# Output projection of the cross-attention by seven products of eight, with block sums of its inputs and its results read back

## The chip, the cores and the metric

The kernel runs on one core of a Trainium2 chip. The metric is the device time of one execution in microseconds. TensorE (PE) multiplies, VectorE (DVE) and ScalarE (ACT) work element by element, GpSimd (POOL) issues some DMAs through its queue and SyncE (SP) issues most of the others. Each engine works through its own queue in order. Activations lie in a shared set of 66 slots in SBUF.

## What is computed

One layer of a hybrid decoder for 512 prompt tokens and 8 single-token samples, 520 columns in all, in float32 with a model width of 2048:

```python
y = mixer(rmsnorm(x, g_mix));          x = x + y          # ends in  @ w_out
q = rmsnorm(x, g_xattn) @ w_cq
o = softmax(q @ mk.T * 512**-0.5) @ mv                    # 4 heads, 256 memory tokens
x = x + o @ w_co                                          # the projection that is changed
x = x + square(relu(rmsnorm(x, g_ffn) @ w_up)) @ w_down
y = rmsnorm(x, g_final)
```

## The kernel before

Columns are tokens (`T` = 520, two halves of `HT` = 260); a tile holds 128 rows of the width, so x is 16 tiles (`KB` = 16). A float32 factor is split into a high and a low part, and each product is three matmuls: high by high, high by low, low by high. A weight tile of 128x1024 (eight 128x128 blocks) is loaded on SP into `wraw`, cast on ACT into `whi` (L129, or L138 in stretches written by hand), and `wlo` = `wraw` - `whi` is made on DVE (L130, L146). `run_jobs` (L164) goes through a list of jobs: it loads the weights of later jobs, splits those of the job after next and then issues the matmuls, with the result's step behind them (`post`).

A plain product (`gemm`, L189) makes a 128x520 tile of results out of 16 input tiles: two jobs of 48 matmuls, 260 columns wide. A quad (`quad_jobs`) makes two such tiles, seen as 2x2 blocks (two input parities by two column halves, two output tiles by two halves), by seven products of eight: sums of weight blocks (`S1` to `S4`, four 128x1024 steps on DVE, L1256), seven products P1 to P7 of 24 matmuls each, and an addition of each product into the results. Its inputs are blocks and sums of blocks of two activation tiles each; those sums are made ahead and split, and part of them is kept in DRAM and loaded at use.

The program in order: the input projection, the mixer; `w_out` as one plain pair (`out_plain`) and seven quads (`out_quad`), whose results go to DRAM (`dx[0]`) and are read back and split (`x1_again`); `w_cq`; then products for keys (`mk_jobs`, L1050) and values (`mv_jobs`, L1081) of four heads, between which the attention of each head (`attn`, L1150) is interleaved, in an order written by hand (`tc.manual_schedule`); `w_co` (`residual`, L858, 16 plain products); the feed-forward with one plain pair, 31 quads of `w_up` and the quads of `w_down`. The cached keys and values of the samples are loaded on POOL and multiplied on DVE meanwhile (L962, L969).

In `attn` each of a head's four outputs lies in PSUM; ACT casts it to `oh` and DVE makes `ol` (L1160). `residual` reads its x tile from `dx[0]`, adds the product (L871), stores it to `dx[1]` and hands it to `fact_out`, which splits it for the up stage (`fa`, L801) and, for every two tiles, makes block sums (L1195) and their split (L1230), stored to `td`. The first two tiles are put off (`put_off`) until the pools of the early stages are closed.

## Time and profile before

| | us |
|---|---|
| runs | 2667.88, 2674.22, 2666.63 (median 2667.88) |
| profiled run, and its span | 2668.74, 2667.0 |
| PE busy in the span | 2639.8 (99%) |
| DVE busy | 2135.2 (80%) |
| ACT busy | 1253.2 (47%) |
| last mk and mv jobs and the attention of the heads | about 943 to 1195 |
| w_co | 1170.2 to 1359.1 |
| up stage's quads | 1383.0 to 2003.7 |

A part of an engine's time counts for the whole only where the others wait for it. So one looks first which engine is busy throughout, then at what it waits for, and then, for another engine, how much it has to do in the stretch in which it gets new work.

### The profile page before, as it was taken

To read this page: it belongs to the slowest core of one execution; us is meant where nothing else is said; L and a number is where in the kernel's file an instruction comes from. 1 tells how busy PE (TensorE), PEld (TensorE's weight loads), DVE (VectorE), ACT (ScalarE), POOL (GpSimd) and SP (SyncE) were. 2 spreads that over 40 slices of the span, in tenths; PEclk is the share of its full clock that TensorE was granted. 3 is DMA by queue.
4 is the path that set the end of the run, shared out by engine and by line. 5 is a ranking of instruction groups with operands and counts; after the bars stand their busy time and mean duration, and the time that the engine had idled before them with its cause. 6 is when DMAs were issued, how large, how long until landed. Compare 5 with 4: busy or idle time off the path is not lost.

```text
span 2667.0 us, 52574 instructions
## 1 busy us (share of the span) xinstructions
PE 2639.8 (99%) x21418; PEld 2602.9 (98%) x21418; DVE 2135.2 (80%) x3593; ACT 1253.2 (47%) x1704; POOL 108.3 (4%) x184
## 2 busy tenths in 40 slices
PE   9999999999999999999999999999999999999997
PEld 9999999999999999989999999999999999999997
DVE  6786786897865567775569999999999998998898
ACT  5646364553453144444445555555553333333344
POOL 0010000000001212110000000000000000000001
PEclk9999999999999999999999999999999999999999
DMA  5354443566456778775566565565579666555642
GB/s 205 105 191 135 124 162 105 177 220 235 141 180 200 274 264 279 264 243 192 184 226 228 195 211 196 190 210 198 189 245 335 217 219 219 180 172 191 212 131 89
DMA packets 236068, 528.91 MB, mean 198 GB/s; under 512 B 24638, under 2 KB 96990, under 8 KB 235826
## 3 DMA queue, kind: packets, MB, share of 16 engines
q1 hardware_dynamic: 216882, 458.43, 51.1%
q0 software_dynamic: 18944, 67.12, 7.3%
q8 instruction: 168, 2.75, 0.4%
q14 instruction: 74, 0.61, 0.1%
HBM read 426.27 MB, written 99.33 MB: 197 GB/s over the span
## 4 chain that ended last, share of the span: by engine, by line
PE 91%; issue 4%; DVE 2%; DMA 2%; ACT 1%; POOL 0%; SPq 0%; POOLq 0%; DVEq 0%; ACTq 0%
PE mm L1286 46%; PE mm L203 29%; PE mm L1050 3%; PE mm L1081 3%; PE aux L222 3%; PE aux L1286 2%; PE mm L1329 2%; DVE wlo L130 1%; PE aux L657 1%; DMA wraw<-in_w_in 1%; PE aux L728 0%; PE aux L661 0%; DMA hc<-r 0%; PE aux L654 0%; DMA wraw<-in_w_mv 0%
## 5 line engine op out<-in xcount | busy, mean ns | idle before, releaser
L129 ACT CAST whi<-wraw 128x1024 fp32r<-128x1024 f32 x396 | 416.0, 1051 | 730.1 <-PE mm L1286 388.2
L1286 PE MATMUL mm<-ha,whi 128*128 128x260 f32 x3584 | 643.5, 283 | 1.9 <-ACT whi L129 1.0
L130 DVE TENSOR_TENSOR wlo<-wraw,whi 128x1024 fp32r<-128x1024 f32 x396 | 483.1, 1220 | 151.3 <-ACT whi L129 149.2
L1286 PEld LDWEIGHTS mm<-ha,whi 128*128 128x128 f32 x3584 | 551.0, 188 | 2.8 <-DVE X L1455 1.3
L1286 PE MATMUL mm<-ha,wlo 128*128 128x260 f32 x1792 | 505.0, 282 | 0.6 <-DVE wlo L130 0.6
L1286 PE MATMUL mm<-ta,whi 128*128 128x260 f32 x2320 | 419.3, 283 | 0.0
L1286 PEld LDWEIGHTS mm<-ta,whi 128*128 128x128 f32 x2320 | 356.2, 188 | 0.0
L1286 PEld LDWEIGHTS mm<-ha,wlo 128*128 128x128 f32 x1792 | 337.0, 188 | 1.0 <-DVE wlo L130 1.0
L1286 PE MATMUL mm<-ta,wlo 128*128 128x260 f32 x1160 | 326.8, 282 | 0.0
L1286 PE MATMUL mm<-fa,whi 128*128 128x260 f32 x1488 | 268.3, 282 | 0.0
L203 PE MATMUL mm<-xh,whi 128*128 128x260 f32 x1280 | 264.2, 287 | 0.9 <-DVE og L775 0.9
L203 PE MATMUL mm<-xl,whi 128*128 128x260 f32 x1280 | 259.9, 284 | 0.0
L203 PE MATMUL mm<-xh,wlo 128*128 128x260 f32 x1280 | 257.8, 282 | 0.0
L1286 PEld LDWEIGHTS mm<-fa,whi 128*128 128x128 f32 x1488 | 228.1, 188 | 0.0
L129 ACT CAST whi<-A 128x1024 fp32r<-128x1024 f32 x126 | 132.3, 1050 | 185.6 <-PE mm L1286 120.2
L138 ACT CAST whi<-wraw 128x1024 fp32r<-128x1024 f32 x100 | 105.1, 1051 | 243.5 <-PE mm L203 84.6
L1286 PEld LDWEIGHTS mm<-ta,wlo 128*128 128x128 f32 x1160 | 218.4, 188 | 0.0
L1286 PE MATMUL mm<-fa,wlo 128*128 128x260 f32 x744 | 209.2, 281 | 0.0
L1455 DVE TENSOR_TENSOR X<-mm,X 128x260 f32<-128x260 f32 x448 | 170.6, 421 | 41.4 <-PE mm L1286 39.5
L203 PEld LDWEIGHTS mm<-xh,whi 128*128 128x128 f32 x1280 | 198.4, 188 | 2.3 <-ACT kv L825 1.0
L203 PEld LDWEIGHTS mm<-xh,wlo 128*128 128x128 f32 x1280 | 198.5, 189 | 0.2
L203 PEld LDWEIGHTS mm<-xl,whi 128*128 128x128 f32 x1280 | 198.0, 189 | 0.3
(420 smaller groups left out, 5093.9 us busy)
## 6 DMA issues: line engine op xcount, KB each, us to landing
ha<-hc SPq DMA_DIRECT2D x224, 260.0 KB
wraw<-in_w_in SPq DMA_DIRECT2D x80, 512.0 KB
wraw<-in_w_up SPq DMA_DIRECT2D x66, 512.0 KB
wraw<-in_w_down SPq DMA_DIRECT2D x64, 512.0 KB
A<-in_w_down SPq DMA_DIRECT2D x64, 512.0 KB
A<-in_w_up SPq DMA_DIRECT2D x62, 512.0 KB
hc<-hhi SPq DMA_DIRECT2D x32, 910.0 KB
hc<-r SPq DMA_DIRECT2D x32, 910.0 KB
```

What stands on the lines that cost most here:

```text
L129: S.copy(hi, raw)
L130: V.tensor_tensor(out=lo, in0=raw, in1=hi.bitcast(F32), op=ALU.subtract)
L138: S.copy(hi, raw)
L203: PE.matmul(ps[:, hf, 0:HT], w[:, j, :], x[:, HALF[hf]], start=(k == 0 and wi == 0), stop=(k == n - 1 and wi == 2))
L222: PE.matmul(out, u, v, start=first and i == 0, stop=last and i == 2)
L657: PE.matmul(nps[:, ms], C[j][:, ms], qs[j][:, cs], start=False, stop=(j == 1))
L1050: PE.matmul(box["ps"], w[:, i, :], x, start=(k == 0 and wi == 0), stop=(k == KB - 1 and wi == 2))
L1081: PE.matmul(box["ps"][:, i], x[:, ms], w[:, j], start=(k == 0 and wi == 0), stop=(k == KB - 1 and wi == 2))
L1286: PE.matmul(out, w[:, j, :], x[:, b], start=(new and k == 0 and wi == 0), stop=(p == LAST[acc] and k == per - 1 and wi == 2), skip_group_c ...
L1329: PE.matmul(ps[mp][:, hf, 0:HT], w[:, j, :], x[hf][:, b], start=(kp == 0 and j == 0 and wi == 0), stop=(kp == 1 and j == 7 and wi == 2))
L1455: V.tensor_tensor(out=x, in0=c, in1=x, op=ALU.add)
```

## The change

`w_co` becomes `projection("w_co", ...)`, the form that `w_out` has already: one plain pair and seven quads. `out_plain`, `out_quad`, `x1_again` and `residual` are replaced by it.

- The heads' outputs are copied from PSUM to a slot `o` on ACT and split by halves into `fo` (`block_out`). Tiles are paired across heads 0 and 1, and 2 and 3. For the four pairs of heads 0 and 1 `o_sums` makes four differences of blocks and their high and low parts and stores them on POOL into `od`, 16 stores; `o_loads` loads them again. For the four pairs of heads 2 and 3 `o_loads` makes the differences and splits them into `to` at the start of the first quad.
- The small SBUF pool is closed two jobs earlier, and the loads of the first quad's four weight tiles (`held`) are issued behind that.
- The results go to `dx[1]`; 14 of the 16 are read back in the last quad, split (`fact_split`), and summed by pairs (`fact_pair`).
- `w_out`'s plain pair reads its inputs in another order, and the weights are packed on the host for both.

```diff
+    def block_diffs(d1, d3, d2, d4, t0, t1):
+        b12, b11, b21, b22 = t0[:, HALF[1]], t0[:, HALF[0]], t1[:, HALF[0]], t1[:, HALF[1]]
+        for out, p, q in ((d1, b12, b11), (d2, b22, d1), (d3, b22, b12), (d4, b21, d2)):
+            V.tensor_tensor(out=out, in0=p, in1=q, op=ALU.subtract)
...
+    def block_out(t, n):
+        fo[n] = [pair_slot("fo") for _ in range(2)]
+        for hf in range(2):
+            split_to(fo[n][hf], t[:, HALF[hf]])
+        if n % 2 == 0:
+            o_even[n // 2] = t
+        elif n < 8:
+            start(o_sums(n // 2, o_even.pop(n // 2), t))
+        else:
+            o_last.append((n // 2, o_even.pop(n // 2), t))
+
+    def o_sums(i, t0, t1):
+
+        yield
+        u, w = slot("ou", (P, 2, HT)), slot("ou", (P, 2, HT))
+        block_diffs(u[:, 0], u[:, 1], w[:, 0], w[:, 1], t0, t1)
+        for k, t in ((0, u), (2, w)):
+            yield
+            hi = pair_slot("oh")
+            S.copy(hi, t)
+            V.tensor_tensor(out=t.bitcast(F32R), in0=t, in1=hi.bitcast(F32), op=ALU.subtract)
+            for b, x in enumerate((hi.bitcast(F32), t)):
+                stream_load(odram[i][k:k + 2, :, b].rearrange("j p c -> p j c"), x)
+
+    def o_loads():
+
+        for i in range(KB // 2):
+            to[i][1], to[i][2], to[i][3] = fo[2 * i][0], fo[2 * i + 1][0], fo[2 * i + 1][1]
+        for j in (6, 4, 5, 7):
+            if j in (6, 4):
+                for i, t0, t1 in o_last[0:2]:
+                    u, w = slot("ou", (P, 2, HT)), slot("ou", (P, 2, HT))
+                    block_diffs(u[:, 0], u[:, 1], w[:, 0], w[:, 1], t0, t1)
+                    for k, x in ((6, w[:, 0]), (4, u[:, 0]), (5, u[:, 1]), (7, w[:, 1])):
+                        to[i][k] = pair_slot("to")
+                        split_to(to[i][k], x)
+                del o_last[0:2]
+            for i in range(len(odram)):
+                to[i][j] = pair_slot("to")
+                load(to[i][j].bitcast(F32), odram[i][j - 4])
+            yield
...
-                hi, lo = slot("oh", dt=F32R), slot("ol", dt=F32R)
-                for src, c in ((op, slice(0, TP)), (od[:, 4 * h + j - 2], DEC)):
-                    S.copy(hi[:, c], src)
-                    V.tensor_tensor(out=lo[:, c], in0=src, in1=hi[:, c].bitcast(F32), op=ALU.subtract)
-                oact.append((hi, lo))
+                t = slot("o")
+                S.copy(t[:, 0:TP], op)
+                S.copy(t[:, DEC], od[:, 4 * h + j - 2])
+                parts.append((t, 8 * (h // 2) + 2 * (j - 2) + h % 2))
...
+    def projection(wname, src, dst, key, facts, tacts, done, again, early):
...
+        def x_done(n):
+            load(dst[n], xs[n])
...
+            if n >= KB - 2:
+                again(xs[n], n)
+            if n % 2:
+                done(n // 2, xs[n - 1], xs[n])
...
+        def read_back():
+            raw = {}
+            for n in range(0, KB, 2):
+                for k in (n, n + 1):
+                    if k < KB - 2:
+                        raw[k] = slot("x1")
+                        load(raw[k], dst[k])
+                if n:
+                    for k in (n - 2, n - 1):
+                        again(raw.pop(k), k)
+                yield
...
+        def evac(m, p, ps):
             n, hf = dict(P1=(0, 0), P2=(0, 0), P6=(0, 1), P5=(1, 1), P7=(1, 1), P3=(0, 1), P4=(1, 0))[p]
...
+            if p in ("P3", "P4"):
+                x_done(2 * m + n)
             if p == "P4" and m == KB // 2 - 2:
-                start(x1_again())
+                start(read_back())
...
-    jobs += residual("w_co", oact, dx[0], dx[1], "ssf", fact_out, lambda: start(block_loads(tact, fact, td, tkept), 2.0))
-    jobs[n_early + 1], jobs[n_early + 2] = jobs[n_early + 2], jobs[n_early + 1]
+    jobs += projection("w_co", dx[0], dx[1], "ssf", fo, to, x2_done, fact_split, False)
+
+    held = [jobs[n_early + 4 + i].pop("fetch") for i in range(2)]
...
+    early_sb.close()
+    late["sb"] = ctx.enter_context(tc.tile_pool(name="late", bufs=2, reuse_waits="tile"))
+    for fetch in held:
+        fetch()
+    start(o_loads())
+    with tc.manual_schedule():
         run_jobs(n_early + 2, n_early + 4, True)
-    early_pools.close()
```

**What moves on DVE in the mk jobs.** This is DVE's queue before, between the low parts (`wlo`) of two weight halves and behind them (`kv` and `sc` are scores with the cached keys, `mk` a result of an mk job):

```order
L146 TENSOR_TENSOR wlo_12995<-wraw_12873,whi_12987 128x1024
L1058 TENSOR_TENSOR mk_12937<-mm_12960,rm_10087 128x256
L146 TENSOR_TENSOR wlo_13027<-wraw_12942,whi_13025 128x1024
L962 ISA kv_12794,sc_12621<-kv_12794,kv_12707 128x512
L962 ISA sc_12621 128x1
```

And the same place now (`mkl` is the low part of the keys, `ou` the differences of blocks of `o`, L891 their low parts; L numbers are those of the changed kernel):

```order
L146 TENSOR_TENSOR wlo_13029<-wraw_12889,whi_13009 128x1024
L1086 TENSOR_TENSOR mk_12953<-mm_12982,rm_10091 128x256
L891 TENSOR_TENSOR ou_13021<-ou_13021,oh_13061 128x520
L817 TENSOR_TENSOR ou_13066<-o_12263 128x260
L817 TENSOR_TENSOR ou_13067<-o_12915,ou_13066 128x260
L817 TENSOR_TENSOR ou_13066<-o_12915,o_12263 128x260
L817 TENSOR_TENSOR ou_13067<-o_12915,ou_13067 128x260
L817 TENSOR_TENSOR ou_13072<-o_12322 128x260
L817 TENSOR_TENSOR ou_13073<-o_12968,ou_13072 128x260
L817 TENSOR_TENSOR ou_13072<-o_12968,o_12322 128x260
L817 TENSOR_TENSOR ou_13073<-o_12968,ou_13073 128x260
L146 TENSOR_TENSOR wlo_13078<-wraw_12958,whi_13059 128x1024
```

One low part and eight differences now stand between `mk` and the next `wlo`; three more low parts and four more differences stand between that one and the `wlo` behind it.

**What moves on DVE at the end of the attention.** Before, behind the last output of head 3 (`ol`), come the weights of the third and fourth job of `w_co` and of the up stage's plain pair, with the first results between them:

```order
L1160 TENSOR_TENSOR ol_14161<-aux_14147,oh_14160 128x512
L1160 TENSOR_TENSOR ol_14161<-od,oh_14160 128x8
L146 TENSOR_TENSOR wlo_14170<-wraw_13920,whi_14168 128x1024
L871 TENSOR_TENSOR x_1992_14221<-mm_13962,xr_13924 128x520
L146 TENSOR_TENSOR wlo_14229<-wraw_14011,whi_14227 128x1024
L1195 TENSOR_TENSOR r_14304<-r_14304 128x260
L871 TENSOR_TENSOR x_1996_14279<-mm_14045,xr_14015 128x520
L130 TENSOR_TENSOR wlo_14321<-wraw_14166,whi_14320 128x1024
```

Now, at the end of the first group of differences and splits (`to`), ahead of the low part of P1's weights:

```order
L798 TENSOR_TENSOR to_14312<-ou_14298,to_14312 128x260
L817 TENSOR_TENSOR ou_14315<-o_14042 128x260
L1281 TENSOR_TENSOR A_2019_14285<-A_2019_14285,A_2021_14289 128x1024
L817 TENSOR_TENSOR ou_14316<-o_14244,ou_14315 128x260
L817 TENSOR_TENSOR ou_14315<-o_14244,o_14042 128x260
L817 TENSOR_TENSOR ou_14316<-o_14244,ou_14316 128x260
L798 TENSOR_TENSOR to_14321<-ou_14316,to_14321 128x260
L798 TENSOR_TENSOR to_14324<-ou_14315,to_14324 128x260
L798 TENSOR_TENSOR to_14327<-ou_14315,to_14327 128x260
L798 TENSOR_TENSOR to_14330<-ou_14316,to_14330 128x260
L146 TENSOR_TENSOR wlo_14341<-wraw_14283,whi_14295 128x1024
L1415 TENSOR_TENSOR xr_14014<-mm_14054,xr_14014 128x520
```

Ahead of these rows stand the weight difference `S`, four differences and three splits; behind them another weight difference and seventeen 260-wide steps stand before the low part of P2's weights.

## Rows read from the trace of the kernel before

**Rows 1.** The page's part 1: engine, busy us, share of the span, instructions.
```profile
PE 2639.8 (99%) x21418; PEld 2602.9 (98%) x21418; DVE 2135.2 (80%) x3593; ACT 1253.2 (47%) x1704; POOL 108.3 (4%) x184
```

**Rows 2.** Groups of PE: line, tiles, shape, count, busy, mean ns; one of three.
```profile
L203 PE MATMUL mm<-oh,whi 128*128 128x260 f32 x512 | 103.0, 282 | 0.0
```

**Rows 3.** Busy time by stretches; the columns stand in the first line.
```profile
core 0: us, PE busy (x) PEld busy (x) DVE busy (x) ACT busy (x) POOL busy (x), PEclk, DMA share, GB/s
1200.00:1250.00 50.00, 50.00 (x421) 50.00 (x420) 27.73 (x44) 22.24 (x35) 0.00 (x0) 1.00 0.60 191
1359.10:1383.00 23.90, 23.90 (x199) 23.78 (x198) 17.41 (x29) 12.60 (x20) 0.00 (x0) 1.00 0.93 339
1383.00:2003.70 620.70, 620.70 (x5210) 620.70 (x5209) 568.97 (x713) 342.23 (x403) 0.00 (x0) 1.00 0.62 207
```

**Rows 4.** The same view: the second quad of w_out and its last.
```profile
633.00:653.10 20.10, 20.10 (x170) 20.10 (x170) 17.01 (x22) 8.64 (x9) 0.00 (x0) 1.00 0.49 152
733.50:753.60 20.10, 20.10 (x171) 20.10 (x170) 19.36 (x28) 15.51 (x20) 0.00 (x0) 1.00 0.75 254
```

**Rows 5.** Groups of DVE instructions: name, shape, count, busy us, mean ns, idle before.
```profile
L871 DVE TENSOR_TENSOR x<-mm,xr 128x520 f32<-128x520 f32 x16 | 11.2, 698 | 50.5 <-PE mm L203 43.3 <-DMA wraw<-in_w_co 7.2
L1230 DVE TENSOR_TENSOR r<-r,hhi 128x1040 fp32r<-128x1040 f32 x6 | 7.5, 1242 | 3.7 <-ACT hhi L1228 3.7
L1160 DVE TENSOR_TENSOR ol<-aux,oh 128x512 fp32r<-128x512 f32 x16 | 10.9, 685 | 12.4 <-ACT oh L1159 12.4
```

**Rows 6.** Waits of PE from 940 to 1200 us: total us, times, longest.
```profile
PE aux L1145 <- DVE p L1132: 1.1, 3, 0.5
PE mm L1081 <- DVE wlo L146: 0.7, 2, 0.5
```

**Rows 7.** Chain of waits, 1060 to 1210 us: start, length, what, count.
```profile
1073.30 22.75 PE mm L1050 x192
1096.06 2.83 PE aux L222 x24
```

**Rows 8.** Timeline of DVE in the mk jobs: start us, us, line, tiles.
```profile
1081.39 0.42 DVE L1037 TENSOR_TENSOR mkl<-mk,mkh 128x256 fp32r<-128x256 f32 x1
1081.73 1.22 DVE L146 TENSOR_TENSOR wlo<-wraw,whi 128x1024 fp32r<-128x1024 f32 x1
1082.87 0.42 DVE L1058 TENSOR_TENSOR mk<-mm,rm 128x256 f32<-128x256 f32 x1
1083.20 1.22 DVE L146 TENSOR_TENSOR wlo<-wraw,whi 128x1024 fp32r<-128x1024 f32 x1
1084.33 0.69 DVE L962 CUSTOM_DVE_ANT_0 kv<-kv,kv 128x512 f32<-128x512 f32 x1
```

**Rows 9.** Busy time by stretches, in the mk jobs.
```profile
1080.00:1090.00 10.00, 10.00 (x87) 10.00 (x86) 8.51 (x18) 4.80 (x7) 3.12 (x5) 1.00 0.79 268
1090.00:1100.00 10.00, 10.00 (x87) 10.00 (x86) 9.46 (x18) 4.81 (x7) 1.28 (x2) 1.00 0.84 299
1100.00:1110.00 10.00, 10.00 (x87) 9.95 (x86) 5.39 (x18) 3.31 (x7) 1.30 (x2) 1.00 0.75 257
```

**Rows 10.** DMA issues, 1060 to 1115 us: tile, queue, count, KB, us to landing.
```profile
kv<-in_V POOLq DMA_DIRECT2D x6, 512.0 KB, 7.1
```

**Rows 11.** Timeline of ACT (ScalarE) in the mk jobs.
```profile
1094.76 1.05 ACT L138 CAST whi<-wraw 128x1024 fp32r<-128x1024 f32 x1 [1.70 <-DMA wraw<-in_w_mk]
```

**Rows 12.** Timeline of DVE at the end of the attention.
```profile
1189.33 0.15 DVE L1160 TENSOR_TENSOR ol<-od,oh 128x8 fp32r<-128x8 f32 x1
1198.90 0.70 DVE L871 TENSOR_TENSOR x<-mm,xr 128x520 f32<-128x520 f32 x1 [1.83 <-PE mm L203]
```

**Rows 13.** Busy time by stretches, at the end of the span.
```profile
2650.00:2655.00 5.00, 3.66 (x21) 2.66 (x19) 4.04 (x11) 2.61 (x6) 4.23 (x6) 1.00 0.28 106
2655.00:2660.00 5.00, 0.00 (x0) 0.00 (x0) 4.49 (x12) 0.38 (x1) 2.29 (x4) 0.71 0.97 368
```

**Rows 14.** Who waited for transfers with tiles named dx: us, times.
```profile
  ACT xah L234: 3.0, 4
```

More of the change, by code (lines that the diff above doesn't have):

```diff
@@ L883, in tile_trunk @@
-    SC = 512.0 ** -0.5
-    xatt, oact = [None] * KB, []
+    SC = 512.0 ** -0.5
+    xatt = [None] * KB
+    fo = [None] * KB
+    to = [[None] * 8 for _ in range(KB // 2)]
+    odram = [dram.tile([4, P, 2, HT], F32, name=f"od{i}") for i in range(KB // 4)]
+    o_even, o_last = {}, []
+    def block_out(t, n):
[8 more added lines that the diff above has]
+            o_last.append((n // 2, o_even.pop(n // 2), t))
@@ L1325, in mm @@
             for j in range(8):
[L1326 removed]
+                x = facts[order(kp, j)]
                 for wi, (w, b) in enumerate(((wh, 0), (wh, 1), (wl, 0))):
@@ L1411, in up_quad, with x_split, x2_done @@
+        return js
+    def x_split(x, n):
+        xatt[n] = split(x, "xa", pc(C_X, n))
+    def x2_done(i, x0, x1):
+        start(fact_pair(i, x0, x1))
+        if i == KB // 2 - 1:
+            start(block_loads(tact, fact, td, tkept), 2.0)
     def up_quad(i):
@@ L1560, in tile_trunk @@
         jobs += gemm(w_in(32 + i), xact, ev_og(i))
-    jobs += out_plain()
-    for m in range(1, KB // 2):
-        jobs += out_quad(m)
+    jobs += projection("w_out", [a["xT"][n] for n in range(KB)], dx[0], "ssx", fy, ty,
+                       lambda i, x0, x1: None, x_split, True)
     for h in range(4):
```

165 lines of the change are left out of this document (62 added, 103 removed).

## The prediction

> **What bounds the kernel now.** I read the busy shares first: TensorE (PE) is busy 99% of the span [rows 1], so a saving must come from its own instructions, and every wait it is newly given counts in full. Then the table by stretches: in the output projection of the attention PE issues 421 matmuls in each 50 us, 118.8 ns apart, at a granted clock of 1.00 (the 2.4 GHz level), while VectorE (DVE) is busy 27.73 of 50 [rows 3]. The waits of PE between 940 and 1200 us come to 1.8 us [rows 6], and between 1195 and 2003 the view lists none. So PE is the bound nearly everywhere, and DVE is the engine to watch: 91.7% busy in the up stage (568.97 of 620.70 us, [rows 3]) and near full in parts of the attention [rows 9].
>
> All sums are made against the profiled run of 2668.74 us (span 2667.0 and 1.7 around it), which lies 0.9 above the median of the runs, 2667.88. About 0.3%, 8.0 us, is what a measurement can tell from no change.
>
> **What it removes.** The 16 plain products of w_co are 3 groups of 512 matmuls, 1536 [rows 2]. After it there are one plain pair (4 jobs of 48, 192) and 7 quads of 7 products of 24 (1176), 1368 together: 168 fewer of the same width, 260. At 118.8 ns [rows 3] that is **20.0 us**. The same sum by the Trainium skill (TensorE: Matmul & The Clock Gate, Back-to-back issue gap) would be 260/2.4 + 2.5 = 110.8 ns, an estimate that makes the gain 18.6 us; the rows here say 118.8, and I keep them.
>
> **What it adds, place by place.** DVE has an in-order queue, so what counts is where the new work stands in it. Starts of consecutive instructions lie about 0.08 us closer than their durations: 0.34 for a 256- or 260-wide block (1081.39 to 1081.73), 1.14 for a weight's low part (1081.73 to 1082.87), 0.61 for a piece of the cached scores (1084.33, 0.69 long) [rows 8], and so by [rows 5] 0.61 for a 520-wide step, 0.60 for a 512-wide one and 1.16 for a 1040-wide one.
>
> *Steady quads.* The same scheme runs already in w_out, where a quad has up to 17.01 us of DVE in 20.1 us, mostly 16.6 ([rows 4] has the highest). A w_co quad has in addition four block sums for the feed-forward (1.36) and their low part (1.16): 16.6 + 2.5 = 19.1 against 168 matmuls x 118.8 ns = 20.0 of PE. I take 0, since w_out's last quad had 19.36 in 20.1 and the waits show none there [rows 4]. If DVE can't be driven above the 91.7% of the up stage, a quad takes 19.1/0.917 = 20.8, 0.9 lost in each of some five: up to 4.3.
>
> *Place A, the block differences of heads 0 and 1.* They are made in the middle of the mk jobs, where PE takes a new weight half of 24 matmuls each 2.84 us (192 in 22.75, [rows 7]) and DVE was busy 8.51, 9.46 and 5.39 of 10 [rows 9]. Added are 16 differences (5.4 us) and 8 low parts of 520 (4.9): 10.3 us. The halves start at 1096.06 less multiples of 2.84 [rows 7]: 1087.5, 1090.4, 1093.2. By the order of the new program, from 1081.39 [rows 8]:
> four differences, mkl, wlo: 1.36 + 0.34 + 1.14, done at 1084.2, needed at 1084.9: no wait.
> mk, one low part, eight differences, wlo: 0.34 + 0.61 + 2.72 + 1.14, done at 1089.0; the third matmul of its half needs it at 1087.7: PE waits 1.3, and ends the half at 1091.6.
> Two pieces of scores 1.22, three low parts 1.83, four differences 1.36, mkl and wlo 1.48: 1094.9, needed at 1091.9: 3.0 more; the half ends at 1097.5.
> mk, three low parts, two low parts of q (1.20), wlo: 4.51, 1099.4, needed at 1097.8: 1.6 more.
> Behind it PE has 24 score matmuls, and the next wlo (about 1104) is in time. **A costs 6.0.** Bounds: 3.7 if every idle piece of DVE can be used up to 1110 (10.3 less the 6.6 that it was idle in the three stretches of [rows 9]), 10.3 if none can. A gain is excluded: nothing is taken off DVE there, since the splits of the outputs take the same time as before (two of 0.34 for one of 0.60 and an 8-wide one).
> The 16 stores (4.3 MB) go through POOL's queue. The stretch moved 268 and 299 GB/s [rows 9]; the most that a row shows is 339 [rows 3], so in 20 us there is room for 1.1 MB, and 3.2 MB (9.3 us at 339) come late. The weights' casts waited for their loads already, up to 1.70 us [rows 11], but that tile was used 9.8 us after its cast was begun at 1094.76 (three groups of 24 behind 1096.06, at 1104.6, [rows 7, 11]). So the 9.3 are just covered: I take 0, and at most 3.3, if A's own stall of 6.0 is all the cover there is. New tiles of q and mk reuse the stores' slots: a store issued at 1085.2 lands by 1092.3 at the 7.1 us of [rows 10], and DVE wants that slot at about 1097: no wait. The loads of V stand behind the stores on POOL; I keep that for rival 4.
>
> *Place B, the start of the first quad.* Between the last attention output and the quad's weights DVE now has the differences and splits of heads 2 and 3. Before, its last output was split at 1189.4 and PE was through the fourth job at 1198.6 (its result is added at 1198.90) [rows 12]. ScalarE now makes a copy and two casts of each output where it made one cast and a small one, so I start DVE at 1190.6 (a choice; 1189.4 to 1192).
> S 1.14, A 1.14, sixteen block steps 5.44, wlo 1.14 gives 1199.5; P1's accumulator is free after one add of 0.61, at 1200.1: PE waits 1.5.
> S2 1.14, seventeen block steps 5.78, wlo of P2 1.14: 1208.2. P1 is over at 1203.0, and P2's third matmul would run at 1203.2: **5.0**.
> Add, wlo of P6: 1209.9, in time. Then a sum of squares, a weight difference, block sums, td's low part, wlo of P5 (0.61 + 1.14 + 1.36 + 1.16 + 1.14): 1215.3, needed at 1213.9: 1.4.
> From there a product costs DVE at most 2.6 for PE's 2.85. **B costs 7.9.** Low 5.0 (P2's wait alone: its 16 splits stand directly ahead of its wlo). High 11: the granted clock fell from 1.00 to 0.71 and on once PE had run out of work at the end [rows 13]; a wait of 5 us may do that in the middle, and 24 matmuls at the 1.2 GHz level would take at most twice their 2.85 us, 2.9 more. The Trainium skill (TensorE: Matmul & The Clock Gate, HAM oscillation) says that waits between bursts of matmuls let the clock drop; no row here shows it with matmuls behind, so B stays at 7.9, and by that rule it would be 10.8.
>
> *Place C, the results.* x2 goes to DRAM and 14 of 16 tiles are read back in the last quad. w_out does this now, and its read-back made ScalarE wait 3.0 us in four places [rows 14], with no wait of PE in the view. Here the last quad and the plain pair behind it have, counted along the order at these durations, about 29.3 us of DVE for 28.8 of PE, and two loads stand on SP behind stores that wait for P3 and P4. I take 1.5 (0 to 5). That w_out's plain pair now reads its inputs in another order costs nothing: its four jobs and their matmuls are the same.
>
> **Sum.** 20.0 - 6.0 - 7.9 - 1.5 = 4.6 faster: 2668.7 - 4.6 = **2664.1**, within 0.3%.
>
> **Rivals.**
> 1. *DVE's lag is mostly absorbed* (faster): A at 3.7, B at P2's wait of 5.0, C at 0: 20.0 - 8.7 = 11.3, so 2657.4. For it: DVE was idle 6.6 us in the stretches of [rows 9], in pieces that a queue running late can use. Against: a half's two products use its wlo from the third matmul on, and the slots for wlo let DVE lead by about 3 us only (1084.3 for 1087.5, [rows 7, 8]). Chance 0.24.
> 2. *All of the 20 us arrives*, 2648.7: needs DVE to hide 10.3 and 19.3 us of work in stretches where PE has 8.4 and 5.7. Chance 0.04.
> 3. *DVE becomes the bound in the steady quads* (slower). w_out's quads show DVE only 16.6 of 20.1 busy, 82.6%. If that share is what its waits on ScalarE and on products leave it, and not PE's pace, a quad takes 19.1/0.826 = 23.1, 3.1 more in each of five: 2664.1 + 15.6 = 2679.7. It decides from 2.5 us a quad on. Against: 91.7% in the up stage and 19.36 of 20.1 in w_out's last quad, without a wait of PE [rows 3, 4]. Chance 0.14.
> 4. *The added 4.3 MB hold up weights or V loads* (A at 10.3 and 3.3 on top, C at 5): 20.0 - 13.6 - 7.9 - 5 = -6.5, so 2675, and with the clock's 2.9 it is 2678. Chance 0.07, of which 0.04 is slower by over 0.3%.
>
> **How the numbers follow.** Forecast (within 0.3%, the rest of the chance) 0.51 and 0.03 of rival 4: same 0.54. Faster 0.24 + 0.04 = 0.28. Slower 0.14 + 0.04 = 0.18. The forecast alone with its bounds (A 3.7 to 10.3, B 5 to 11, C 0 to 5, quads 0 to 4.3, not all at one end) is 2657 to 2673. The range for 8 in 10 is 2655 to 2676: it takes in rival 1 and leaves out rivals 2 and 3.
>
> **What would show it.** Right: PE's waits name wlo (L146) between 1085 and 1100 with about 6 us, and again some 8 us at the first quad's P1, P2 and P5, the second of these the longest; DVE 10 of 10 through both; no wait of PE in quads two to six, DVE at 19 of 20. Wrong: waits on DMAs or whi at A (rival 4), waits spread over the quads (rival 3), or DVE's queue full while PE's waits stay under 9 us (rival 1). The whole would be wrong if the spacing of the 168 matmuls saved were not theirs, that is if the stretch of w_co took other than 1368 x 118.8 = 162.5 us plus the waits named.

## The result and the profile after

The changed kernel takes 2674.39 us (median of 20 runs) beside 2670.26 for the kernel before in the same runs: a ratio of 1.0015, 95% interval 1.0009 to 1.0021, about 4 us slower. It lies inside the range and within the 0.3%, but the forecast was 4.6 us faster; the sign was wrong, and the interval excludes the forecast.

The table compares two traces of each kernel, cut into stages by the first and last start of the matmuls of each stage's tiles (the view of one tile's instructions); all is in us. The stage "keys, values, attention" runs from the first mk job to the last attention matmul; "behind it" from there to the first quad of the up stage, nearly all of it `w_co`:

| | first quad of w_out starts at | keys, values, attention | behind it | up stage | down stage |
|---|---|---|---|---|---|
| before | 612.9 | 245.7 | 196.1 | 620.8 | 646.9 |
| before, second trace | 615.0 | 244.9 | 196.1 | 620.8 | 646.8 |
| after | 615.1 | 254.3 | 187.6 | 622.5 | 647.5 |
| after, second trace (m2) | 613.7 | 254.5 | 187.8 | 622.5 | 647.5 |

With nothing lost, "behind it" would be 196.1 - 20.0 = 176.1. So the 20.0 us were gained and given back: 8.6 in the attention (place A), 11.5 at the first quad (place B). What is left is 1.7 in the up stage, 0.6 in the down stage and 2.2 ahead of w_out, by which the two traces of before differ as well.

First the page's part 1, which answers to [rows 1]: 168 matmuls fewer, DVE 84.7 us more, and PE's share now 98%.

```profile
PE 2631.6 (98%) x21250; PEld 2594.4 (97%) x21250; DVE 2219.9 (83%) x3733; ACT 1295.1 (48%) x1781; POOL 119.7 (4%) x200
```

The waits of PE between 1080 and 1260 us (total, times, longest), which answer to [rows 6]. L1078 are the mk jobs, L1311 the quads:

```profile
PE mm L1078 <- DVE wlo L146: 5.4, 3, 2.9
PE mm L1311 <- DVE wlo L146: 3.7, 1, 3.7
PE mm L1311 <- DVE xr L1415: 2.2, 1, 2.2
PE mm L1311 <- ACT whi L129: 1.1, 1, 1.1
PE aux L222 <- DVE mvl L1065: 0.8, 1, 0.8
PE aux L1173 <- DVE p L1160: 0.5, 1, 0.5
```

The waits for `wlo` at A and at P2 and the one for the addition ahead of P1 (`xr`) stand where the prediction put them. The third at the first quad does not: it lies at 1232.01, ahead of P7, where the prediction had one for P5's `wlo` (the products run in the order P1, P2, P6, P5, P7, P3, P4). From there to the end of the up stage the view names no other. The busy times by stretches (columns as in [rows 3]; these answer to [rows 9] and [rows 4]) show what the waits don't:

```profile
1080.00:1090.00 10.00, 9.41 (x79) 9.20 (x78) 9.47 (x23) 7.12 (x16) 2.05 (x4) 1.00 0.49 160
1090.00:1100.00 10.00, 5.20 (x38) 4.79 (x37) 9.93 (x22) 5.20 (x9) 4.12 (x6) 0.95 0.92 318
1100.00:1110.00 10.00, 10.00 (x76) 9.92 (x76) 10.00 (x19) 5.09 (x8) 4.84 (x7) 0.88 0.86 276
1210.00:1220.00 10.00, 5.14 (x27) 4.94 (x28) 9.69 (x22) 5.91 (x13) 0.00 (x0) 0.76 0.41 133
1220.00:1230.00 10.00, 10.00 (x64) 9.97 (x65) 9.18 (x13) 4.88 (x7) 0.00 (x0) 0.73 0.81 259
1260.00:1280.00 20.00, 20.00 (x170) 20.00 (x169) 18.95 (x26) 10.96 (x14) 0.00 (x0) 1.00 0.65 212
1340.00:1360.00 20.00, 20.00 (x169) 20.00 (x169) 19.58 (x37) 17.64 (x32) 0.00 (x0) 1.00 0.75 253
```

DVE is full at A. In the three stretches there PE issued 193 matmuls where it had issued 261 [rows 9]: 68 fewer, 8.1 us at 118.8 ns, of which the waits are 5.4. Between 1220 and 1230 PE is "busy" throughout and yet issues 64 instead of 86: the granted clock is 0.73. PE's timeline shows it matmul by matmul, at A and at the first quad (start, length, what, count, idle before); the last four rows, two of them of DVE, are read further below, under k1:

```profile
1092.95 0.39 PE L1078 MATMUL mm<-mh,wlo 128*128 128x256 f32 x1 [1.93 <-DVE wlo L146]
...
1098.95 0.51 PE L1078 MATMUL mm<-mh,wlo 128*128 128x256 f32 x1 [2.87 <-DVE wlo L146]
...
1103.46 0.39 PE L1078 MATMUL mm<-mh,wlo 128*128 128x256 f32 x1
...
1211.17 0.51 PE L1311 MATMUL mm<-fo,whi 128*128 128x260 f32 x2 [2.22 <-DVE xr L1415]
...
1212.22 0.64 PE L1311 MATMUL mm<-fo,whi 128*128 128x260 f32 x2
...
1212.87 0.64 PE L1311 MATMUL mm<-fo,whi 128*128 128x260 f32 x2
...
1215.32 0.40 PE L1311 MATMUL mm<-fo,whi 128*128 128x260 f32 x2
...
1215.68 0.40 PE L1311 MATMUL mm<-fo,whi 128*128 128x260 f32 x2
...
1219.76 0.58 PE L1311 MATMUL mm<-fo,wlo 128*128 128x260 f32 x1 [3.68 <-DVE wlo L146]
...
1224.13 0.42 DVE L1423 TENSOR_TENSOR x<-mm,x 128x260 f32<-128x260 f32 x1
1224.69 0.73 PE L1311 MATMUL mm<-to,whi 128*128 128x260 f32 x2
...
1231.49 0.42 DVE L1423 TENSOR_TENSOR x<-mm,x 128x260 f32<-128x260 f32 x1
1232.01 0.48 PE L1311 MATMUL mm<-to,whi 128*128 128x260 f32 x2 [1.07 <-ACT whi L129]
```

Behind the wait of 2.22 three matmuls take 0.65 us (1212.22 to 1212.87), 216.7 ns each instead of 118.8: the 1.2 GHz level. By 1215.32 three take 0.36 us again. The same in the granted clock, in stretches of 4 us:

```profile
1212.00:1216.00 4.00, 4.00 (x22) 3.87 (x21) 3.69 (x11) 3.73 (x8) 0.00 (x0) 0.61 0.98 321
1220.00:1224.00 4.00, 4.00 (x19) 4.00 (x20) 4.00 (x7) 1.26 (x2) 0.00 (x0) 0.50 0.68 212
1100.00:1104.00 4.00, 4.00 (x25) 3.92 (x25) 4.00 (x8) 2.13 (x4) 2.43 (x4) 0.69 0.78 254
```

The slow matmuls took this much longer, from the starts: the 24 from 1211.17 to 1215.68 took 4.51 us where 24 x 118.8 ns is 2.85, 1.7 more; the 22 from 1219.76 to 1224.69 took 4.93 instead of 2.61, 2.3 more; at A the 16 from 1098.95 to 1102.47 (256 wide, about 213 ns apart) took 3.52 instead of 1.90, 1.6 more. Whether this adds to the kernel's time, or only fills time in which PE would have waited, is settled below, under k1.

### The profile page after: what moved, and what is told of

It is laid out like the page before. It is cut to its first block, busy times and chain, and to the rows that moved or that the text cites. A ratio compares the mean times of both kernels' runs of the same rounds, so it can differ in the third digit from the quotient of the medians.

```text
span 2671.9 us, 52641 instructions
## 1 busy us (share of the span) xinstructions
PE 2631.6 (98%) x21250; PEld 2594.4 (97%) x21250; DVE 2219.9 (83%) x3733; ACT 1295.1 (48%) x1781; POOL 119.7 (4%) x200
## 4 chain that ended last, share of the span: by engine, by line
PE 89%; DVE 4%; issue 4%; ACT 1%; DMA 1%; POOL 0%; SPq 0%; POOLq 0%; DVEq 0%; ACTq 0%
PE mm L1311 53%; PE mm L203 22%; PE mm L1109 3%; PE mm L1078 3%; PE aux L222 2%; PE aux L1311 2%; PE mm L1354 2%; DVE wlo L130 1%; PE aux L657 1%; PE aux L728 0%; PE aux L661 0%; DMA out_rh<-hs 0%; DVE wlo L146 0%; DVE ou L817 0%; PE aux L654 0%
## 5 line engine op out<-in xcount | busy, mean ns | idle before, releaser
L1311 PE MATMUL mm<-ha,whi 128*128 128x260 f32 x3584 | 644.5, 283 | 1.6 <-ACT whi L129 1.0
L130 DVE TENSOR_TENSOR wlo<-wraw,whi 128x1024 fp32r<-128x1024 f32 x396 | 483.2, 1220 | 132.6 <-ACT whi L129 131.1
L1311 PEld LDWEIGHTS mm<-ha,whi 128*128 128x128 f32 x3584 | 550.9, 188 | 2.4 <-ACT whi L129 1.2
L1311 PE MATMUL mm<-ha,wlo 128*128 128x260 f32 x1792 | 504.9, 282 | 0.5 <-DVE wlo L130 0.5
L1311 PE MATMUL mm<-ta,whi 128*128 128x260 f32 x2320 | 419.6, 283 | 0.0
L1311 PEld LDWEIGHTS mm<-ta,whi 128*128 128x128 f32 x2320 | 356.7, 188 | 0.0
L1311 PEld LDWEIGHTS mm<-ha,wlo 128*128 128x128 f32 x1792 | 337.3, 188 | 1.0 <-DVE wlo L130 0.9
L1311 PE MATMUL mm<-ta,wlo 128*128 128x260 f32 x1160 | 327.2, 282 | 0.0
L1311 PE MATMUL mm<-fa,whi 128*128 128x260 f32 x1488 | 269.7, 283 | 0.0
L129 ACT CAST whi<-A 128x1024 fp32r<-128x1024 f32 x140 | 147.0, 1050 | 193.8 <-PE mm L1311 135.5
L1311 PEld LDWEIGHTS mm<-fa,whi 128*128 128x128 f32 x1488 | 228.4, 188 | 0.0
L1311 PEld LDWEIGHTS mm<-ta,wlo 128*128 128x128 f32 x1160 | 218.1, 188 | 0.0
L1311 PE MATMUL mm<-fa,wlo 128*128 128x260 f32 x744 | 209.3, 281 | 0.0
```

Source lines behind the costliest of these rows:

```text
L129: S.copy(hi, raw)
L130: V.tensor_tensor(out=lo, in0=raw, in1=hi.bitcast(F32), op=ALU.subtract)
L1311: PE.matmul(out, w[:, j, :], x[:, b], start=(new and k == 0 and wi == 0), stop=(p == LAST[acc] and k == per - 1 and wi == 2), skip_group_c ...
```

## The experiments

L numbers in the answers are those of each kernel. All times are medians beside the kernel before on the same chip; stages as in the table above.

| | time, us | ratio to before, 95% | keys, values, attention | behind it | up stage |
|---|---|---|---|---|---|
| e1 no DVE work at A | 2676.42 | 1.0023 [1.0014, 1.0032] | 256.5 | 188.3 | 623.7 |
| e2 no stores at A | 2671.80 | 1.0010 [1.0001, 1.0018] | 254.0 | 187.8 | 622.0 |
| e3 no work at B | 2662.48 | 0.9970 [0.9958, 0.9981] | 253.9 | 177.3 | 622.7 |
| e4 e1 and e3 | 2658.83 | 0.9956 [0.9944, 0.9969] | 254.2 | 177.6 | 622.1 |
| e5 neither at A | 2664.49 | 0.9984 [0.9975, 0.9993] | 246.3 | 188.1 | 621.5 |
| m1 e5 and e3 | 2650.84 | 0.9929 [0.9916, 0.9943] | 248.3 | 177.7 | 620.0 |
| k1 clock held up at B | 2673.51 | 1.0018 [1.0009, 1.0026] | 255.7 | 188.0 | 622.5 |
| f1 sums one pair at a time | 2671.24 | 1.0004 [0.9995, 1.0013] | 251.0 | 188.0 | 621.6 |
| f2 each block made at its use | 2670.43 | 1.0005 [0.9996, 1.0014] | 253.9 | 185.4 | 621.9 |
| f3 a second plain pair | 2672.40 | 1.0009 [1.0000, 1.0018] | 254.1 | 185.4 | 623.7 |
| g4 sums later and slower, and f2 | 2663.48 | 0.9979 [0.9970, 0.9988] | 246.8 | 186.0 | 623.3 |
| g2 the same, and f3 | 2665.03 | 0.9986 [0.9977, 0.9995] | 246.6 | 185.8 | 621.6 |

### What holds PE up at place A

**e1** leaves out the sixteen differences and eight low parts, and with them ACT's eight casts for them; the 16 stores stay.

```diff
-        block_diffs(u[:, 0], u[:, 1], w[:, 0], w[:, 1], t0, t1)
...
-            V.tensor_tensor(out=t.bitcast(F32R), in0=t, in1=hi.bitcast(F32), op=ALU.subtract)
-            for b, x in enumerate((hi.bitcast(F32), t)):
-                stream_load(odram[i][k:k + 2, :, b].rearrange("j p c -> p j c"), x)
+            for b in range(2):
+                stream_load(odram[i][k:k + 2, :, b].rearrange("j p c -> p j c"), fo[2 * i + b][k // 2].bitcast(F32))
```

> The changed kernel with the four block differences and two high and low parts of each pair of heads 0 and 1 left out: the same 16 stores to od, from tiles that exist already, so DVE is relieved of 10.3 us and ACT of 8 casts at place A, and the DMA work stays. My theory (the trace of the changed kernel: PE waits 5.4 us for wlo at A and 0.8 us later, and runs 16 matmuls at the half clock level behind the last wait, 1.5 us): 7.7 us less than the changed kernel, about 2666.7. Rival (the 4.3 MB of stores hold up the weights): no change, about 2674.

My theory fell: no gain at all, 256.5 us of attention. PE ran through the mk jobs without a wait, and then stood in the values' jobs instead. The rows are two stretches, the timelines of POOL and of DVE, and a wait of PE in e1, and as the last row a load of V in the changed kernel:

```profile
1080.00:1110.00 30.00, 30.00 (x257) 29.96 (x256) 24.36 (x52) 14.46 (x25) 10.30 (x15) 1.00 0.89 295
1120.00:1130.00 10.00, 3.22 (x9) 2.24 (x8) 6.95 (x19) 2.17 (x4) 4.79 (x8) 0.66 0.84 276
...
1117.69 0.72 POOL L960 DMA_DIRECT2D kv<-in_V  x1 [3.27 <-issue]
...
1123.02 0.42 DVE L992 CUSTOM_DVE_ANT_0 kv<-kv,kv 128x256 f32<-128x256 f32 x1 [7.62 <-DMA kv<-in_V]
...
PE mm L1104 <- DVE wlo L146: 6.8, 1, 6.8
...
1116.60 0.72 POOL L965 DMA_DIRECT2D kv<-in_V  x1 [1.29 <-issue]
```

The loads of V stand behind the stores in POOL's queue. The kernel before issues them at 1084.27, 1088.96, 1096.73 and 1103.22; e1 at 1087.25 and then only at 1117.69, with gaps named "issue" between the stores. DVE's queue reaches the scores that need that load, waits 7.62 us, and the `wlo` behind it is late for PE. The changed kernel issues the same load nearly as late, at 1116.60, but there DVE comes to those scores later still and doesn't wait for it.

**e2** keeps the DVE work and leaves the stores out (the loads read the twin tensor of w_out instead).

```diff
-            for b, x in enumerate((hi.bitcast(F32), t)):
-                stream_load(odram[i][k:k + 2, :, b].rearrange("j p c -> p j c"), x)
...
-                load(to[i][j].bitcast(F32), odram[i][j - 4])
+                load(to[i][j].bitcast(F32), ydram[i][j - 4])
```

> The changed kernel with all of DVE's and ACT's work at place A, but without the 16 stores; the later loads read another DRAM tensor of the same form (yd). My theory: DVE's queue is the cause, so at most 1 us less than the changed kernel, 2673 to 2675. Rival (stores): 7 to 8 us less, about 2666.7.

The attention takes 254.0, and PE's waits are those of the DVE work:

```profile
1095.95 0.39 PE L1076 MATMUL mm<-mh,wlo 128*128 128x256 f32 x1 [1.48 <-DVE wlo L146]
...
1100.45 0.38 PE L1076 MATMUL mm<-mh,wlo 128*128 128x256 f32 x1 [1.38 <-DVE wlo L146]
...
1216.77 0.58 PE L1309 MATMUL mm<-fo,wlo 128*128 128x260 f32 x1 [5.21 <-DVE wlo L146]
```

At A they come to 5.4 us in four waits, of 0.59, 1.93, 1.48 and 1.38; the last row, at P2, is for k1 below. So either cause alone costs the whole loss. **e5** leaves out both; its loads read the twin tensor as in e2.

```diff
-            start(o_sums(n // 2, o_even.pop(n // 2), t))
+            o_even.pop(n // 2)
```

> Neither the differences nor the 16 stores at place A (the later loads read yd in their place); B as in the changed kernel. The runs before this one showed that DVE's work alone (no stores) and the stores alone (no DVE work: V loads 20 us late on POOL, DVE waits 7.6 us for one) each lose 8 to 11 us between the start of the mk jobs and the last attention matmul. Theory of two causes, each enough: with both gone that stretch is back at 245.7 us, as in the kernel before, and the time 8.5 below the changed kernel, about 2666. Rival (a third cause in that stretch, the copies to o and the splits by halves, which stay): 2670 or more.

The attention takes 246.3, where before has 245.7 and 244.9, and the second load of V goes out at 1088.45 again. Two sufficient causes, one hidden behind the other: that is why e1 gained nothing.

### What place B costs

**e3** leaves out the differences and splits of heads 2 and 3; the products read other tiles.

```diff
-                    block_diffs(u[:, 0], u[:, 1], w[:, 0], w[:, 1], t0, t1)
-                    for k, x in ((6, w[:, 0]), (4, u[:, 0]), (5, u[:, 1]), (7, w[:, 1])):
-                        to[i][k] = pair_slot("to")
-                        split_to(to[i][k], x)
+                    for k, x in ((6, 1), (4, 0), (5, 2), (7, 3)):
+                        to[i][k] = fo[2 * i + x // 2][x % 2]
```

> The changed kernel with the differences and splits of the last four pairs (heads 2 and 3) left out, tiles that exist already taken in their place: 32 block steps of DVE and 16 casts of ACT less at place B. My theory: the waits of PE at the first quad (2.2, 3.7 and 1.1 us) go, and the 40 to 45 matmuls at the half clock level behind them (4.1 us) too: 11 us less than the changed kernel, about 2663.3. Rival (the quad's weights, not the differences, are late at B, since their loads were moved): under 3 us less, 2671 or more.

Confirmed: 177.3, 10.3 us less than after, against 176.1 without any loss. **e4** joins e1 and e3:

> Both left out, at A and at B. My theory that these two places and the clock hold nearly all of the loss: 18.8 us less than the changed kernel, about 2655.6. If the loss at the two places is all there is and the 168 matmuls are worth 20.0 us, it is 20 below the kernel before, 2650.3; a time above 2656 means that some 4 us were lost in stages that the change does not name.

It came 3.2 us above what was expected: the stores still hold up the V loads, PE waits 4.2 us there, and the attention takes 254.2.

**m1** joins e5 and e3, **m2** is the changed kernel again.

> Both added pieces of work are left out: neither the block differences, their low parts, the stores and their loads of heads 0 and 1 (place A), nor the differences and splits of heads 2 and 3 (place B; the products read other tiles instead, so the output is not the reference's). Theory: the lost 20 us are A and B alone, each on its own, and they add. Then the attention takes about 246.3 us (as with A left out alone), the stretch from the last attention matmul to the up stage about 177.4 (as with B left out alone), together 18 us less than before, no wait of PE named wlo at either place, granted clock 1.00 at both, and with 1 to 2 us of up stage on top about 2653. Rival: the two hide part of each other (what A delays, B would have waited for), then the stretch behind the attention comes out longer than 180 and the time at 2657 or more. The up stage itself: 620.8 as in both traces of before if its extra 0.7 to 2.9 us came from the added work, 621.5 or more if it came from where the changed program puts its tiles.

> The changed kernel once more, for a second trace. If the up stage's spacing belongs to the kernel, the up stage takes 622.5 us again within 0.2; if it belongs to the run, anything from 620.8 to 623.7. The attention and the stretch behind it come again at 254 and 188 us if the waits of PE for wlo are the kernel's own; time about 2674.

m1 is 2650.84, 18.0 below before: with the added work gone, nearly all of the 20.0 arrives. The two losses add (248.3 and 177.7), so they don't hide each other. The attention was expected at 246.3: of the 2.0 more, 1.2 is longer waits of PE for low parts of weights, at 977 and 981 us, ahead of A; why they are longer isn't shown. A wait of 1.0 for an addition is left at the first quad, and the clock is whole there; compare the same stretch of after:

```profile
PE mm L1303 <- DVE x L1415: 1.0, 1, 1.0
...
1210.00:1220.00 10.00, 9.50 (x79) 9.50 (x80) 8.89 (x12) 4.43 (x6) 0.00 (x0) 1.00 1.03 368
```

m2 gives 622.5 for the up stage again, so its length belongs to the kernel; 620.0 in m1 fits the added work as its cause, but 621.5 to 623.7 in e1, e3, e4 and e5, each with a part of it, doesn't order by the work. **b1**, the kernel before again, was run for the same question:

> The kernel before, once more, for a second trace of it. In every kernel with the change so far the up stage, whose code is the same, took 621.5 to 623.7 us, and in the one trace of the kernel before 620.8. If that 0.7 to 2.9 is an effect of the change, this trace shows 620.8 again; if it is the spread between runs, 621.5 or more. The same for the stretch up to w_out's first quad, 612.3 to 615.1 in all traces, with the changed kernel's at 615.1.

It took 2669.97 and 620.8 in the up stage, as in the first trace.

### What the clock costs at B

**k1** lets PE multiply zeros where it would stand: 18 matmuls ahead of P1 into a spare bank, 28 in P2 ahead of its first use of `wlo`, added to the accumulator as zeros.

```diff
+                        if fill and p == "P2" and k == 0 and wi == 1:
+                            for _ in range(28):
+                                PE.matmul(out, w[:, j, :], late["zero"], start=False, stop=False, skip_group_check=True)
...
+                for _ in range(18):
+                    PE.matmul(t[:, 0:HT], wh[:, 0, :], late["zero"], start=True, stop=True)
```

> The changed kernel with matmuls of zeros put into the two waits of PE at place B: 18 of them ahead of P1 (2.1 us at the 2.4 GHz level, the wait was 2.2) and 28 between P2's second and third matmul (3.3 us, the wait was 3.7). They change no result and no other engine. In the changed kernel some 19 matmuls of P1 and 25 of P2 and P6 stand 216.7 ns apart behind these waits, where 118.8 is the rule. Theory (the clock fell because PE stood still, and that is 4.1 us of B's loss): granted clock 1.00 through 1200 to 1240, 4 us less than the changed kernel, about 2670. Rival (the spacing has another cause, or the zeros only lengthen the queue): 2674 or more.

There was no gain. These are PE's timeline, a row of DVE and two stretches of 4 us in k1:

```profile
1209.69 2.32 PE L1322 MATMUL aux<-zero,whi 128*128 128x260 f32 x18
1212.07 0.51 PE L1311 MATMUL mm<-fo,whi 128*128 128x260 f32 x2
...
1215.27 3.52 PE L1316 MATMUL mm<-zero,whi 128*128 128x260 f32 x28
1220.66 0.39 PE L1311 MATMUL mm<-fo,wlo 128*128 128x260 f32 x1 [1.86 <-DVE wlo L146]
...
1225.03 0.42 DVE L1436 TENSOR_TENSOR x<-mm,x 128x260 f32<-128x260 f32 x1
1225.55 0.48 PE L1311 MATMUL mm<-to,whi 128*128 128x260 f32 x2 [0.47 <-issue]
...
1212.00:1216.00 4.00, 3.94 (x34) 3.93 (x34) 3.68 (x10) 3.95 (x8) 0.00 (x0) 1.00 0.76 239
1220.00:1224.00 4.00, 3.34 (x17) 3.34 (x18) 4.00 (x5) 1.26 (x2) 0.00 (x0) 0.66 0.48 145
```

P1 ran whole at 2.4 GHz: its 24 matmuls took 2.97 us (1212.07 to 1215.04) where they took 4.51 in the changed kernel, 1.5 less, and PE waited that much longer for P2's `wlo`. Then the zeros ran out 1.86 us early and the clock fell in P2 all the same. e2 is a second case: there P1 ran whole without any zeros, behind a wait of 2.19, and the wait at P2 was 5.21 instead of 3.68. The starts of the first quad's products, in us behind the last attention matmul of each kernel, with the number of slow matmuls in P1 and P2:

| | after | m2 | e2 | k1 |
|---|---|---|---|---|
| P1's first matmul | 13.39 | 13.40 | 13.47 | 13.43 |
| slow matmuls in P1 | 15 | 15 | 0 | 0 |
| P2's third matmul, the first with `wlo` | 21.98 | 22.00 | 22.06 | 22.03 |
| slow matmuls in P2 | 21 | 20 | 17 | 15 |
| P6's first matmul | 26.91 | 27.01 | 26.95 | 26.91 |
| P7's first matmul | 34.24 | 34.25 | 34.32 | 34.40 |

The starts are the same to 0.2 us, however many matmuls ran slow. What sets them is DVE: at P2 its `wlo`, and at P6 and P7 an addition. P6 and P7 are summed in the same accumulator as P1 (`ACC`, x for P1, P6, P7 and P4), so P6 can begin only when DVE has added P1's result, and P7 when it has added P6's. In all four traces each begins 0.10 to 0.14 us behind the end of that addition (in after 1224.13 + 0.42, then PE at 1224.69; 1231.49 + 0.42, then PE at 1232.01). In k1 PE stands 0.47 us ahead of P6; in after the view shows no wait there, because the slow matmuls of P2 end just as the addition does. The `whi` that the view names at P7 isn't what decides there: in m2 the same wait is given as 0.89 "issue", again 0.10 behind the addition.

The same holds at A. In the changed kernel the fourth `wlo` is late too, but no wait is listed at 1103.46: 16 slow matmuls stand in its place. In e2 the clock falls one half earlier and the slow matmuls stand in place of part of the third wait (1.48 instead of 2.87), and the fourth is seen (1.38). Over the 140 matmuls of this place the loss is 7.8 to 7.9 us in both, in m2, and in k1, f2, f3 and e3 too. So the lower clock costs these kernels next to nothing at either place: its matmuls ran while PE would otherwise have waited for DVE.

### Versions that spread the work

**f1** makes the sums of heads 0 and 1 one pair after the other instead of overlapping.

```diff
+    def o_serial():
+        for _ in range(KB // 4):
+            while not o_queue:
+                yield
+            yield from o_sums(*o_queue.pop(0))
...
-            start(o_sums(n // 2, o_even.pop(n // 2), t))
+            o_queue.append((n // 2, o_even.pop(n // 2), t))
```

> The changed kernel with the sums of the four pairs of heads 0 and 1 made one pair after the other, one step in each job, over some 12 jobs of 2.8 us, where it made all four at once in some four jobs. The same work and the same stores, 0.9 us of DVE a job. Theory of two causes: both get room, A loses 2 us at most, so about 2668 (2666 to 2670). Rival (the stores on POOL hold up the V loads however they are spaced, since at most a few are under way at a time): the loss stays, 2673 or more.

The loss at A falls from 8.6 to 5.3, less than its theory said (2 at most) and more than its rival (no change): PE still waits 1.9 us for `wlo` of the keys' and values' jobs and 2.0 for `p` between 1080 and 1260 us. **f2** makes, ahead of P1, only the blocks that P2 needs, and each of the others ahead of the product that reads it:

```diff
+        for c, (i, t0, t1) in enumerate(o_last):
+            u, w = slot("ou", (P, 2, HT)), slot("ou", (P, 2, HT))
+            ou.append((u, w))
+            V.tensor_tensor(out=u[:, 0], in0=t0[:, HALF[1]], in1=t0[:, HALF[0]], op=ALU.subtract)
+            V.tensor_tensor(out=w[:, 0], in0=t1[:, HALF[1]], in1=u[:, 0], op=ALU.subtract)
+            tile_(i, 6, w[:, 0])
```

> The changed kernel with the work at place B in the order in which the products want it: for P6 two differences and one split of each pair, then the split for P5, the difference and split for P7, those for P4, one group in each job, instead of all of two pairs in each of two jobs. The same work in all. Theory (DVE's queue ahead of the low parts of P1's and P2's weights): 4.7 us less of DVE ahead of P2's weights, waits at P1 and P2 under 2 us each, and no half clock behind them: 5 to 8 us less than the changed kernel, 2667 to 2670. Rival (the quad has 30 us of DVE work for 20 of PE in any order, so the loss only moves to P5, P7 and the second quad): within 2 us of it.

B is 2.2 us better where 5 to 8 were hoped for, which is nearer to the rival. One long wait is left, 2.9 for P2's `wlo`, then 0.8 at P6 behind the addition, and the clock still falls (0.58 from 1210 to 1220). **f3** puts a second plain pair (4 more jobs of 48, 24 matmuls more than the quad it replaces) between the attention and the first quad:

```diff
-    jobs += projection("w_co", dx[0], dx[1], "ssf", fo, to, x2_done, fact_split, False)
+    jobs += projection("w_co", dx[0], dx[1], "ssf", fo, to, x2_done, fact_split, False, 2)
```

> The changed kernel with two plain pairs of w_co and six quads: 24 matmuls more (2.9 us), and the differences of heads 2 and 3 are made during the second plain pair, in which DVE has some 6 us of other work in 22.8. Theory: B's 10.3 us go and 2.9 come, 7 us less than the changed kernel, about 2667. Rival (what is lost at B is lost wherever the first quad begins): 2677, slower by the 2.9.

It did not reach the 2667 hoped for: the wait moved with the quad. The differences were begun only in the second pair, and DVE, idle over half the stretch before, was full behind it:

```profile
1200.00:1210.00 10.00, 10.00 (x85) 10.00 (x85) 4.30 (x7) 4.46 (x7) 0.00 (x0) 1.00 0.47 168
1220.00:1230.00 10.00, 10.00 (x86) 10.00 (x85) 10.00 (x23) 5.78 (x13) 0.00 (x0) 1.00 1.04 355
1240.00:1250.00 10.00, 6.01 (x36) 5.88 (x37) 5.47 (x9) 2.55 (x4) 0.00 (x0) 0.83 0.81 277
...
PE mm L1311 <- DVE x L1423: 4.2, 1, 4.2
```

The wait of 4.2 is the one ahead of P6, named here for the addition that it waits for.

**g4** begins the sums of heads 0 and 1 four jobs later, makes one step in every second job, and has f2's order at B:

```diff
+    def o_serial():
+        for _ in range(4):
+            yield
+        for _ in range(KB // 4):
+            while not o_queue:
+                yield
+            for _ in o_sums(*o_queue.pop(0)):
+                yield
+                yield
+            yield
```

> The changed kernel with the sums of heads 0 and 1 one pair after the other, one step in every second job and four jobs later (over some 25 jobs, to about 1180), and the differences at the first quad in the order of the products, as in the run with that alone. In the run with one step in each job the stretch from the mk jobs to the last attention matmul took 251.0 us (before: 245.7, changed: 254.3), in the lazy run the rest up to the up stage 185.4 (changed: 187.6). Theory: 248 and 185.4, so 8.5 less than the changed kernel, about 2666. Rival (DVE and POOL have no room in the mv jobs either): 251 or more, 2669.

**g2** is g4 with f3's second pair, its differences begun in the first:

> As the one before, with two plain pairs of w_co and the differences of heads 2 and 3 begun during the first of them and ended during the second. Theory: PE has 45.6 us of plain products over which 10.9 us of DVE are spread, so no wait and no half clock at the first quad: 248 and 176.1 + 2.9 + 1 = 180 up to the up stage, together 14 less than the changed kernel, about 2660, below the kernel before by 9. Rival (the second plain pair's own 5 us of waits on DVE, seen with two pairs alone, stay): 2665.

Both clear A (246.8 and 246.6), at less cost on POOL too: g4 issues the V loads at 1088.48, 1092.63, 1100.81 and 1108.35. g4 is 0.21% faster than before, interval 0.12 to 0.30%, and 0.36% faster than after by the two ratios. It beats both kernels, and its own forecast of about 2666 by more than 2 us. g2 came out where its rival put it, at 2665. B's remaining loss shows in waits of PE in g4, and in two rows of the timelines of g2:

```profile
PE mm L1344 <- DVE wlo L146: 2.4, 1, 2.4
PE mm L1344 <- issue: 1.5, 1, 1.5
...
1233.70 0.43 DVE L1456 TENSOR_TENSOR x<-mm,x 128x260 f32<-128x260 f32 x1 [2.69 <-DMA x<-dx]
1234.23 0.48 PE L1344 MATMUL mm<-to,whi 128*128 128x260 f32 x2 [3.87 <-issue]
```

g2's wait of 3.87 is the one ahead of P6 again: PE begins 0.10 us behind the addition of P1's result, and DVE had stood 2.69 us ahead of that addition, for the load of x from `dx`. This wait is the largest part of what keeps g2 behind the 2660 that its theory gave, which had the 2.9 of the 24 added matmuls in it already.

## Why the prediction was wrong

What bounds the kernel and where the change would hurt were right; the lag of DVE was worked out too small. The step that failed is the following of DVE's queue against PE, most of all at the first quad, in "Add, wlo of P6: 1209.9, in time": P6 waits not only for its `wlo` but for the addition of P1's result, which frees the accumulator, and that addition stands on DVE behind a sum of squares, a weight difference and three block sums. It cost 2.3 us that the sum had at nothing. At A the queue began later than was assumed. What each step worked out and what the trace of the changed kernel shows, as starts of PE later than they would have been without it, in us:

| step | worked out | after |
|---|---|---|
| A, first half | 0 | 0.8 |
| A, second half | 1.3 | 2.2 |
| A, third half | 3.0 | 3.1 |
| A, fourth half | 1.6 | 1.7 |
| B, P1 | 1.5 | 2.4 |
| B, P2 | 5.0 | 5.5 |
| B, P6 | 0 | 2.3 |
| B, P5 or P7 | 1.4 | 1.6 |

- **The gain of 20.0** was right. 168 matmuls are gone [rows 1 and the page of after], and m1 gets 18.0 of it.
- **A, 6.0**: the four halves add up to 5.9 as they were worked out, and to 7.8 as measured. The prediction let DVE begin the first four differences at 1081.39. It began them at 1084.82, which is 1082.5 on before's time axis (after is 2.36 us later there already, from stretches ahead of A), behind splits of outputs of which two had waited 0.85 and 0.46 for ACT. So the first `wlo` was done 1.2 us later than worked out, and the slack of 0.7 that it was given was gone. From there on the queue ran as worked out: the four `wlo` start 5.04, 6.01 and 4.50 us apart, for 4.81, 5.89 and 4.51. A wait also costs 0.2 to 0.3 more than its listed length: at P2 the starts stand 3.96 apart (1215.80 to 1219.76) where the wait is listed as 3.68 and the spacing is 0.12. The other 0.8 of the stage's 8.6 lies outside these halves, most of it a wait of 0.8 for `mvl` that e5 and m1 have too.
- **The stores, 0 to 3.3**: this step was wrong. I priced them by bandwidth and kept the V loads behind them for rival 4 with 0.07. e1 and e4 show that this queue alone costs as much as the DVE work does. It didn't add to the time of after, because DVE was late there anyway, so the 0 came out by luck; the reason given for it (cover of ACT's casts) was the wrong one.
- **B, 7.9**: the stage lost 11.5. By the table 2.3 of the 3.6 that were missing are P6's, 0.9 P1's, 0.5 P2's and 0.2 the later product's, which adds up to 0.3 more than the stages give. The last size was right for another wait: not P5's `wlo` but the addition of P6's result held up PE, ahead of P7. The loss is a little over the high end of 11.
- **The clock**: it fell, and B stayed at 7.9 without it. The Trainium skill (TensorE: Matmul & The Clock Gate, HAM oscillation) says that waits between bursts let the clock drop; this case's trace agrees, with 0.61 and 0.50 granted in the stretches behind the waits of 2.2 and 3.7 us. But the 2.9 that the prediction would have added by it, to 10.8, are not borne out as a cost of their own: after, e2 and k1 reach P2, P6 and P7 at the same times with different numbers of slow matmuls. That 10.8 lies near 11.5 is chance, and to leave the clock out was right for a reason that the prediction did not give.
- **C, 1.5**: it cost 0; there is no wait of PE in the last quad or the up stage's first pair, with DVE 19.58 of 20.
- **The steady quads, 0**: this was right, with DVE at 18.95 of 20, no wait and 170 matmuls in 20 us. Rival 3 falls.
- **Rival 1** (6.6 us of idle DVE absorbs part) falls: DVE was full and PE lost more than was worked out. f1 and g4 show that the idle time can be used, but only when the sums are spread over more jobs. **Rival 2** isn't what the change does, but m1 shows that it was DVE and POOL that stood in its way.
- The sum of the profiled runs: forecast 4.6 faster, found 4.9 slower, 9.5 apart: A 2.6, B 3.6, C -1.5, up and down stages 2.3, 2.2 ahead of w_out that before shows too, 0.3 in the rest. The prediction had no term for the up and down stages, and the cause of their 2.3 stays open. In the up stage it is 1.7 us, without a wait of PE and at a granted clock of 1.00, 839 matmuls in 100 us instead of 841:

```profile
1600.00:1700.00 100.00, 100.00 (x839) 100.00 (x839) 91.41 (x116) 55.17 (x65) 0.00 (x0) 1.00 0.59 198
1600.00:1700.00 100.00, 100.00 (x841) 100.00 (x841) 91.66 (x116) 55.20 (x65) 0.00 (x0) 1.00 0.59 199
```

The first row is after's, the second before's. It repeats in the same kernel (622.5 twice, 620.8 twice) and differs between kernels that run the same instructions there; which of their tiles' places or which work ahead of it decides it wasn't settled.

## What to carry to other kernels

When PE is the bound, price a burst of new work on an in-order engine by where it is queued, and follow that queue to everything that PE waits for behind it: not the weights alone, but also the additions that free an accumulator for the next product. Don't add matmuls at a lower clock to such waits as a cost of their own while the engine that feeds PE is late: here they stood in place of the next wait. To tell, compare when PE starts, not what the view lists as waits. Ask of every queue that the change adds to which loads stand behind its new entries: two causes can each be sufficient, and taking out the one that the wait names then gains nothing. Work that isn't due for a hundred microseconds belongs in small steps between the urgent ones: the same sums, begun four jobs later and made one step in every second job, together with blocks made only ahead of their use, turned the loss into a gain.
